# Hybrid decoder block on one core: the written order of scores and projections on TensorE, and who splits the weights beside them

## The chip, the cores and the metric

The kernel runs on one core of a Trainium2 chip, as one program. The metric is device time in microseconds (us) from start to end of the program. TensorE (PE in the profile) does the matmuls, VectorE (DVE), ScalarE (ACT) and GpSimd (POOL) work elementwise, and SyncE (SP) issues most transfers.

## What is computed

One layer of a decoder trunk on x of 512 tokens by 1024 channels: an input projection feeds three mixers and three gates, each mixer's output is projected, gated and summed, an output projection and a LayerNorm follow, then a squared-ReLU MLP and a second LayerNorm. The mixers are MoBA block attention (A), a chunked gated delta rule (B) and sparse attention over tokens that an indexer selects (C). The change lies in the indexer, which in the reference comes down to:

```
qi, ki, wi = columns of the input projection    # 8 heads x 64, one shared key of 64, 8 weights
ki    = layer_norm(ki)
score = sum over heads h of  wi[t,h] * scale * relu(qi[t,h] . ki[s])
top_k(score, causal) -> the tokens that query t may see in branch C
```

Everything is float32, and the matmuls reach that precision by splitting each operand into two halves.

## The kernel before

**Halves.** A weight tile (1024 x 128) comes in by a transfer on SP's queue into `wraw`, ScalarE rounds it to the high half `wh`, and `wl = wraw - wh` is the low half. `mm3` then makes three matmuls for each 128 rows of the weight, high x high, high x low and low x high: a triple (lines 92 to 94). Eight triples are one tile of projection, 128 output columns for all 512 tokens. `wraw`, `wh` and `wl` have three buffers each.

**Who subtracts.** `split` (line 76) counts its calls: each adds `share[0]` to `share[1]`, and the call at which the sum comes to 1 gives its subtraction to GpSimd and takes 1 off again. All other calls give it to VectorE. `share[0]` is 0 while x is loaded, is set to `SHARE[0]` = 0.34 at line 220 (every third call goes to GpSimd), and takes the next entries of `SHARE`, 0.67 among them, at later stages.

**Order.** A `Stream` holds the projection tiles in order: two of the indexer's queries (`qi`), two of `k_b`, two `qi`, two `k_b`, four `q_b`, then `v_b` and `z_b` in turn. `weave(steps, n)` runs a list of steps and puts the triples of the next n tiles between them, evenly. When a tile's last triple is through, its own elementwise work follows: `q_stack` for `qi` (two `qs` operations on VectorE), a convolution for `k_b` and `q_b` (three `y` operations on VectorE), and, after the fourth of a kind, a sigmoid and a product on GpSimd (line 282).

**The indexer's loop** (lines 431 to 440) has four weaves, each with one tile and six steps (two heads, three blocks of queries). A step, `index_score`, makes two matmuls into one of two `sc` banks (`q` with `kih`, line 318, then with `kil`, line 319; 256, 384 or 512 columns), ScalarE takes the ReLU into one of two `irl` buffers (line 423), and VectorE weights it and adds it to `isc` (line 428). Between two scores stand one or two triples. After the first weave come small matmuls, and rows of a bias table are sent to memory in 3 MB from ScalarE's queue (`rrep`). The key `kin` is normalised before that: variance, a power -0.5 on GpSimd (`krs`, line 264), four scalings (line 392), a transpose on TensorE, and `kih` and `kil` from it.

**Who sets the order.** The program is written as one list. A scheduler then orders each engine's instructions by its own estimates, within the dependences, so the order on an engine can differ from the written one, except in a `manual_schedule` block, where the named engines keep the written order. The loop is not in such a block before.

**Later.** The delta rule runs four chunks of a recurrence. A chunk takes norms with the power on GpSimd (`ss`), scales its output on VectorE (`o`, line 700), turns the next keys (`kn`, line 657) and gives them back to TensorE (line 662). Splits go on there at the share of that stage, and so they do in both attentions and the MLP.

Of the kernel before, what the change touches and what calls it, by code (L numbers as in the profile page):

```python
# [10 lines left out]
F32 = mybir.dt.float32  # L11
F32R = mybir.dt.float32r
AF = mybir.ActivationFunctionType
OP = mybir.AluOpType
# [5 lines left out]
NT = T // 128  # L20
# [18 lines left out]
SHARE = (0.34, 0.67, 0.67, 0.34, 0.34)  # L39
# [16 lines left out]
def hybrid_block(ctx, tc, xT, xn, wt, wva, wsm, wuk, wuv, wbr, wout, wup, wdn, relb, onehot, cmats,  # L56
                 convw, alog, dtb, gnorm, kvnorm, ikg, ikb, l1g, l1b, l2g, l2b, out):
    nc = tc.nc
    PE, DVE, ACT, POOL = nc.tensor, nc.vector, nc.scalar, nc.gpsimd
# [4 lines left out]
    const = ctx.enter_context(tc.tile_pool(name="const", bufs=1))  # L64
# [5 lines left out]
    def bank(tag):  # L70
        return ps.tile([128, 512], F32, name=tag, tag=tag, bufs=BANKS[tag])


    share = [0.0, 0.0]
# [8 lines left out]
    def load_w(src):  # L83
        raw = wp.tile([128, 1024], F32, name="wraw", bufs=3)
        nc.sync.dma_start(raw, src)
        h = wp.tile([128, 1024], F32R, name="wh", bufs=3)
        l = wp.tile([128, 1024], F32R, name="wl", bufs=3)
        split(h, l, raw)
        return h, l
# [9 lines left out]
    def load_x(u, n=2):  # L99
        raw = wp.tile([128, 1024], F32, name="wraw", bufs=3)  # L100
        for k in range(0, 2, n):
            s = slice(2 * u + k, 2 * u + k + n)
            rs = slice(512 * k, 512 * (k + n))
            nc.sync.dma_start(raw[:, rs], xT[:, 512 * s.start:512 * s.stop])
            split(xh[:, s].rearrange("p a t -> p (a t)"), xl[:, s].rearrange("p a t -> p (a t)"), raw[:, rs])
# [11 lines left out]
    class Stream:  # L117
# [27 lines left out]
        def weave(self, steps, n):  # L145
            self.taken += n
            start, end = self.pos, self.ends[self.taken - 1] if self.taken else 0.0
            for i, f in enumerate(steps):
                f()
                self.upto(start + (end - start) * (i + 1) / len(steps))  # L150
            self.upto(end)

    stream = Stream()
    weave = stream.weave
# [62 lines left out]
    load_x(1)  # L217
    load_x(2)
    load_x(3)
    share[0] = SHARE[0]  # L220

    cm = const.tile([128, len(CN), 128], F32, name="cm")
    for i, j in ((0, 4), (4, len(CN))):
# [1 line left out]
    C = {n: cm[:, i] for i, n in enumerate(CN)}  # L225
# [89 lines left out]
    def scores(q, a, k, l, i, n):  # L315
        p = bank("sc")
        ts = slice(128 * i, 128 * i + 128)
        PE.matmul(p[:, :n], q[:, a, ts], k[:, :n], start=True, stop=False)
        PE.matmul(p[:, :n], q[:, a, ts], l[:, :n], start=False, stop=True)
        return p  # L320
# [5 lines left out]
    def t5_rows():  # L326


        rrow = ip.tile([16, NR], F32, name="rrow", bufs=1)
        p = bank("sc")  # L330
        PE.matmul(p[:16, :NR], rbt, ohs, start=True, stop=True)
        ACT.activation(rrow, p[:16, :NR], AF.Copy, bias=0.0, scale=-1.0)
        nc.scalar.dma_start(rrep, rrow[:, None, :].to_broadcast([16, 128, NR]))
# [5 lines left out]
    p = bank("pj")  # L339
# [6 lines left out]
    p = bank("tr")  # L346
# [28 lines left out]
    la = gat[:, 5]  # L375
# [15 lines left out]
    for i in range(NT):  # L391
        DVE.tensor_scalar(kin[:, i, :64], sm[:, i, :64], kag[:, i, 0:1], krs[:, i:i + 1],
                          op0=OP.subtract, op1=OP.mult)
# [4 lines left out]
    p = bank("tr")  # L398
# [20 lines left out]
    def index_score(h, i):  # L419
        n = 128 * (i + 1)  # L420
        p = scores(qis[h // 2], h % 2, kih, kil, i, n)
        rl = ip.tile([128, T], F32, name="irl")
        ACT.activation(rl[:, :n], p[:, :n], AF.Relu)
        w = wis[:, i, h:h + 1]
        if h == 0:
            DVE.tensor_scalar(isc[i], rl[:, :n], w, None, op0=OP.mult)
        else:
            DVE.scalar_tensor_tensor(isc[i], rl[:, :n], w, isc[i], op0=OP.mult, op1=OP.add)

    weave([], 1)  # L430
    for j in range(4):
        weave([lambda h=h, i=i: index_score(h, i) for h in (2 * j, 2 * j + 1) for i in range(1, NT)], 1)
        if j == 0:
            p = bank("tr")
            PE.matmul(p[:, 0:16], C["le"], la, start=True, stop=True)
            PE.matmul(p[:, 16:32], C["gt"], la, start=True, stop=True)
            ege = const.tile([128, 3, 16], F32, name="ege")
            ACT.activation(ege[:, 0:2].rearrange("p a c -> p (a c)"), p[:, :32], AF.Exp)
            DVE.tensor_scalar(ege[:, 2], ege[:, 0], -1.0, None, op0=OP.mult)
            t5_rows()  # L440


    weave([], 4)
# [546 lines left out]
    def hid():  # L990
        return (fin.tile([128, T], F32R, name="hh", bufs=KH + 1), fin.tile([128, T], F32R, name="hl", bufs=KH + 1))
# [23 lines left out]
    for k in range(8):  # L1015
        if k < 3:
            h, l = load_w(wout[k])
# [4 lines left out]
        for a in range(2):  # L1022
            h, l = hid()
# [60 lines left out]
    for half in range(2):  # L1084
# [13 lines left out]
        for f in range(f0, KH):  # L1098
            w = load_w(wup[half * KH + f])
            p = bank("pj")  # L1100
            up_cols(p, w, 0, T)
            hid_t.append(act2(p))
        for a in range(2):
# [44 lines left out]
            for t in range(NT):  # L1148
                ts = slice(128 * t, 128 * t + 128)
                n = 512 // len(pd[t])  # L1150
                for i, p in enumerate(pd[t]):
                    for k in range(8):
                        h = hid_t[2 * lead + k]
# [78 lines left out]
```

## Time and profile before

| | us |
|---|---|
| time, median of 3 runs | 986.3 (986.23 to 987.13) |
| the profiled execution, its own time | 987.62 |
| its span in the trace | 985.8 |
| TensorE busy | 957.7 |
| VectorE, ScalarE, GpSimd busy | 548.6, 429.5, 282.3 |

The mean clock granted to TensorE in the profiled execution is 0.994 of full speed. A row of a timeline reads: start, duration, engine, line, operation, output <- inputs, shape, count, and in brackets how long the engine stood idle just before and what ended that. Matmuls overlap each other in the records, so the distance of two starts, not the duration, says what one takes.

### The profile page before, as it was taken

The numbers are of one execution on the slowest core, as the hardware profiler recorded it, in microseconds if no ns is written. First come the engines' busy times: TensorE is split into PE (matmuls) and PEld (weight loads), VectorE is DVE, ScalarE is ACT, GpSimd is POOL, SyncE is SP. The second block draws the span as 40 slices with busy tenths as digits, with TensorE's granted clock in tenths as the row PEclk, the third lists the DMA queues.
The fourth block names the chain that finished last, engine by engine and source line by source line (L and its number), as shares of the span: only waits on it lengthen the run. The fifth ranks groups of instructions, "written<-read, shape, count | busy, mean of one in ns | idle before, by whom it ended". The sixth has DMA issues, their size and how long they took to land.

```text
span 985.8 us, 12962 instructions
## 1 busy us (share of the span) xinstructions
PE 957.7 (97%) x4868; PEld 791.5 (80%) x4868; DVE 548.6 (56%) x1108; ACT 429.5 (44%) x780; POOL 282.3 (29%) x190
## 2 busy tenths in 40 slices
PE   7999999999989999999999999999999999999997
PEld 4768888887878888877878878988888888888886
DVE  4966648778988556687766666732313123231327
ACT  4445446433224766888863440244421214342210
POOL 0202335300123233255436241154320123432011
PEclk9999999999999999999999999999999999999999
DMA  6375322342113522434436554333232223232322
GB/s 203 129 106 146 112 86 67 126 149 97 44 55 107 150 70 75 113 92 113 128 109 203 181 177 177 107 109 106 89 103 90 103 86 107 88 105 88 105 64 86
DMA packets 39211, 109.65 MB, mean 111 GB/s; under 512 B 5324, under 2 KB 10093, under 8 KB 39149
## 3 DMA queue, kind: packets, MB, share of 16 engines
q1 hardware_dynamic: 37084, 105.69, 32.8%
q10 hardware_dynamic: 2064, 3.15, 2.6%
q8 instruction: 38, 0.62, 0.3%
q14 instruction: 25, 0.20, 0.1%
HBM read 93.09 MB, written 11.53 MB: 106 GB/s over the span
## 4 chain that ended last, share of the span: by engine, by line
PE 60%; DVE 5%; ACT 3%; issue 1%; POOL 0%; DMA 0%; DVEq 0%; ACTq 0%; POOLq 0%
PE pj L92 14%; PE pj L94 14%; PE pj L93 14%; PE sc L92 2%; PE sc L94 2%; PE sc L93 2%; PE tr L92 1%; PE tr L94 1%; PE tr L93 1%; PE tr L778 1%; PE ov L92 1%; PE ov L93 1%; PE ov L94 1%; ACT wh L77 1%; PE ov L797 1%
## 5 line engine op out<-in xcount | busy, mean ns | idle before, releaser
L77 ACT CAST wh<-wraw 128x1024 fp32r<-128x1024 f32 (+2 forms) x144 | 147.8, 1026 | 207.6 <-PE pj L93 85.6
L81 POOL TENSOR_TENSOR wl<-wraw,wh 128x1024 fp32r<-128x1024 f32 (+2 forms) x50 | 116.3, 2326 | 295.5 <-ACT wh L77 295.3
L81 DVE TENSOR_TENSOR wl<-wraw,wh 128x1024 fp32r<-128x1024 f32 (+2 forms) x94 | 116.5, 1241 | 149.2 <-ACT wh L77 148.8
L92 PE MATMUL pj<-xh,wh 128*128 128x512 f32 (+1 forms) x472 | 192.9, 409 | 0.6 <-ACT xh L77 0.3
L94 PE MATMUL pj<-xh,wl 128*128 128x512 f32 (+1 forms) x472 | 186.5, 395 | 2.4 <-DVE wl L81 2.4
L93 PE MATMUL pj<-xl,wh 128*128 128x512 f32 (+1 forms) x472 | 186.0, 394 | 1.8 <-DVE xl L81 1.8
L94 PEld LDWEIGHTS pj<-xh,wl 128*128 128x128 f32 (+1 forms) x472 | 88.7, 188 | 23.1 <-DVE wl L81 3.7
L92 PE MATMUL pj<-x1h,wh 128*128 128x512 f32 (+1 forms) x280 | 104.0, 371 | 0.0
L93 PE MATMUL pj<-x1l,wh 128*128 128x512 f32 (+1 forms) x280 | 103.8, 371 | 0.0
L94 PE MATMUL pj<-x1h,wl 128*128 128x512 f32 (+1 forms) x280 | 103.8, 371 | 0.0
L93 PEld LDWEIGHTS pj<-xl,wh 128*128 128x128 f32 (+1 forms) x472 | 88.9, 188 | 17.2 <-DVE xl L81 3.9
L92 PEld LDWEIGHTS pj<-xh,wh 128*128 128x128 f32 (+1 forms) x472 | 88.8, 189 | 17.2 <-ACT xh L77 1.6
L1081 DVE TENSOR_TENSOR hl<-hraw,hh 128x512 fp32r<-128x512 f32 x32 | 22.2, 692 | 108.3 <-ACT hh L1080 108.3
L1078 POOL TENSOR_TENSOR hraw<-hraw 128x512 f32<-128x512 f32 x32 | 44.3, 1384 | 60.2 <-ACT hraw L1077 60.2
L94 PEld LDWEIGHTS pj<-x1h,wl 128*128 128x128 f32 x280 | 52.7, 188 | 9.1
L93 PEld LDWEIGHTS pj<-x1l,wh 128*128 128x128 f32 x280 | 52.7, 188 | 9.0
L92 PEld LDWEIGHTS pj<-x1h,wh 128*128 128x128 f32 x280 | 52.7, 188 | 9.0
L1080 ACT CAST hh<-hraw 128x512 fp32r<-128x512 f32 x32 | 19.9, 622 | 70.2 <-POOL hraw L1078 70.2
L763 ACT ACTIVATE P<-P,ast 128x128 f32<-128x128 f32 (+1 forms) x64 | 36.1, 564 | 19.5 <-DVE ast L762 19.1
L784 DVE TENSOR_TENSOR ptl<-tr,pth 128x128 fp32r<-128x128 f32 (+1 forms) x64 | 31.1, 487 | 10.0 <-ACT pth L783 9.1
L758 POOL TENSOR_TENSOR bm<-strip,isc 128x256 f32<-128x256 f32 (+2 forms) x24 | 26.2, 1094 | 30.3 <-DVE ast L762 20.2
L778 PE MATMUL tr<-cm,P 128*128 128x128 f32 x160 | 28.2, 275 | 1.4 <-DVE ast L764 1.3
(373 smaller groups left out, 1955.0 us busy)
## 6 DMA issues: line engine op xcount, KB each, us to landing
wraw<-in_wt_dram SPq DMA_DIRECT2D x58, 512.0 KB, 3.4
wraw<-in_wup_dram SPq DMA_DIRECT2D x32, 512.0 KB, 3.3
wraw<-in_wdn_dram SPq DMA_DIRECT2D x32, 512.0 KB, 3.3
gdram<-gate SPq DMA_DIRECT2D x24, 256.0 KB, 2.0
wraw<-in_wbr_dram SPq DMA_DIRECT2D x12, 512.0 KB, 3.7
g<-gdram SPq DMA_DIRECT2D x24, 256.0 KB, 2.9
khl<-khl SPq DMA_DIRECT2D x16, 256.0 KB, 3.7
wraw<-in_wout_dram SPq DMA_DIRECT2D x8, 512.0 KB, 3.8
```

Source lines behind the costliest of these rows:

```text
L77: ACT.copy(h, raw)
L81: eng.tensor_tensor(l, raw, h.bitcast(F32), OP.subtract)
L92: PE.matmul(out_ap, lh, rh, start=first, stop=False)
L93: PE.matmul(out_ap, lh, rl, start=False, stop=False)
L94: PE.matmul(out_ap, ll, rh, start=False, stop=last)
L758: POOL.tensor_tensor(bm[:, :n], bias, self.masks[i], OP.add)
L763: ACT.activation(P, P, AF.Exp, bias=mi[:, 0:1], scale=-1.0, accum_out=mi[:, 2:3])
L778: PE.transpose(pt[:, 128 * j:128 * j + 128], self.P[:, c:c + 128], ident)
L784: DVE.tensor_tensor(dest(self.ptl), pv, dest(self.pth).bitcast(F32), OP.subtract)
L1078: POOL.tensor_tensor(a, a, a, OP.mult)
L1080: ACT.copy(th, a)
L1081: DVE.tensor_tensor(tl, a, th.bitcast(F32), OP.subtract)
```

## The change

Two edits. The indexer's loop goes into a `manual_schedule` block for TensorE, so that TensorE keeps the order in which scores and triples are written. And the line that sets the share to 0.34 moves from behind the loads of x to behind the loop: the splits that are called in between (eight of them) all go to VectorE. Lines of the changed kernel stand one lower than before up to the loop, and two higher behind it.

```diff
     load_x(3)
-    share[0] = SHARE[0]
...
     weave([], 1)
-    for j in range(4):
-        weave([lambda h=h, i=i: index_score(h, i) for h in (2 * j, 2 * j + 1) for i in range(1, NT)], 1)
-        if j == 0:
...
+    with tc.manual_schedule(engines={mybir.EngineType.PE}):
+        for j in range(4):
+            weave([lambda h=h, i=i: index_score(h, i) for h in (2 * j, 2 * j + 1) for i in range(1, NT)], 1)
+            if j == 0:
...
+                t5_rows()
+    share[0] = SHARE[0]
```

TensorE in the loop, before, where scores come again after thirteen triples without any (`sc` is a score's bank, `pj` the bank of a tile of projection):

```order
L318 MATMUL sc<-kih,qs 128x256
L319 MATMUL sc<-kil,qs 128x256
L318 MATMUL sc<-kih,qs 128x384
L319 MATMUL sc<-kil,qs 128x384
L92 MATMUL pj<-xh,wh 128x512
L318 MATMUL sc<-kih,qs 128x512
L319 MATMUL sc<-kil,qs 128x512
L93 MATMUL pj<-xl,wh 128x512
L318 MATMUL sc<-kih,qs 128x256
L319 MATMUL sc<-kil,qs 128x256
L94 MATMUL pj<-xh,wl 128x512
```

The same stretch of the changed kernel:

```order
L317 MATMUL sc<-kih,qs 128x384
L318 MATMUL sc<-kil,qs 128x384
L92 MATMUL pj<-xh,wh 128x512
L93 MATMUL pj<-xl,wh 128x512
L94 MATMUL pj<-xh,wl 128x512
L317 MATMUL sc<-kih,qs 128x512
L318 MATMUL sc<-kil,qs 128x512
L92 MATMUL pj<-xh,wh 128x512
L93 MATMUL pj<-xl,wh 128x512
L94 MATMUL pj<-xh,wl 128x512
L317 MATMUL sc<-kih,qs 128x256
L318 MATMUL sc<-kil,qs 128x256
```

Before, nine scores stood ahead of the thirteen triples and fifteen behind them, with single projection matmuls between; now whole triples stand between any two scores, all along the loop.

VectorE ahead of the loop, before, at the key's normalisation (`rs_v` is the variance that GpSimd's power reads, `kin` the scaled key, `gat` and `wis` small operands of other work):

```order
L373 TENSOR_SCALAR gat<-gat 128x16
L263 TENSOR_SCALAR rs_v<-kag 128x4
L406 TENSOR_SCALAR wis<-sm 128x32
L392 TENSOR_SCALAR kin<-sm,kag,krs 128x64 x3
L364 TENSOR_SCALAR gat<-gat 128x16
```

The same place in the changed kernel:

```order
L372 TENSOR_SCALAR gat<-gat 128x16
L262 TENSOR_SCALAR rs_v<-kag 128x4
L81 TENSOR_TENSOR wl<-wraw,wh 128x1024
L391 TENSOR_SCALAR kin<-sm,kag,krs 128x64
L363 TENSOR_SCALAR gat<-gat 128x16
```

A split that stood on GpSimd ahead of the power now stands on VectorE between `rs_v` and the scaling.

GpSimd in the recurrence, before (`ss` is the power of a chunk, `Sd` the decayed state):

```order
L684 TENSOR_TENSOR Sd<-S,el 128x512
L264 TENSOR_TENSOR ss<-rs_v,cvals 128x4
L684 TENSOR_TENSOR Sd<-S,el 128x512
L264 TENSOR_TENSOR ss<-rs_v,cvals 128x4
L81 TENSOR_TENSOR wl<-wraw,wh 128x1024
L264 TENSOR_TENSOR ss<-rs_v,cvals 128x4
L81 TENSOR_TENSOR wl<-wraw,wh 128x1024
L264 TENSOR_TENSOR ss<-rs_v,cvals 128x4
```

GpSimd in the recurrence of the changed kernel:

```order
L81 TENSOR_TENSOR wl<-wraw,wh 128x1024
L686 TENSOR_TENSOR Sd<-S,el 128x512
L263 TENSOR_TENSOR ss<-rs_v,cvals 128x4
L686 TENSOR_TENSOR Sd<-S,el 128x512
L263 TENSOR_TENSOR ss<-rs_v,cvals 128x4 x2
L81 TENSOR_TENSOR wl<-wraw,wh 128x1024
L263 TENSOR_TENSOR ss<-rs_v,cvals 128x4
```

The count of `split` reaches 1 at other calls from the loop on, so one split now stands ahead of the first `Sd`, and none between the second and the third `ss`; the one between the third and the fourth stays. Over the whole program 51 of 163 splits stand on GpSimd, where it was 54.

## Rows read from the trace of the kernel before

**Rows 1.** The page, busy time (share of the span) and instructions of each engine.

```profile
PE 957.7 (97%) x4868; PEld 791.5 (80%) x4868; DVE 548.6 (56%) x1108; ACT 429.5 (44%) x780; POOL 282.3 (29%) x190
```

**Rows 2.** Stretches: length, busy PE, PEld, DVE, ACT, POOL, PEclk, DMA share, GB/s.

```profile
70.00:80.00 10.00, 9.71 (x39) 8.03 (x39) 8.09 (x14) 5.80 (x12) 0.00 (x0) 0.83 0.90 104
280.00:290.00 10.00, 9.46 (x57) 8.60 (x58) 8.65 (x18) 2.21 (x9) 0.00 (x0) 0.83 0.33 107
300.00:590.00 290.00, 283.33 (x1495) 235.24 (x1494) 195.01 (x441) 190.14 (x402) 108.29 (x79) 1.00 0.41 125
```

**Rows 3.** Timeline of TensorE in the indexer's loop.

```profile
42.27 0.39 PE L319 MATMUL sc<-kil,qs 128*128 128x256 f32 x1 [1.38 <-DVE kil L404]
...
63.02 0.39 PE L93 MATMUL pj<-xl,wh 128*128 128x512 f32 x1
63.25 0.39 PE L94 MATMUL pj<-xh,wl 128*128 128x512 f32 x1
...
63.59 0.28 PE L319 MATMUL sc<-kil,qs 128*128 128x256 f32 x1
63.70 0.34 PE L318 MATMUL sc<-kih,qs 128*128 128x384 f32 x1
63.88 0.34 PE L319 MATMUL sc<-kil,qs 128*128 128x384 f32 x1
64.06 0.39 PE L92 MATMUL pj<-xh,wh 128*128 128x512 f32 x1
...
70.29 0.79 PE L318 MATMUL sc<-kih,qs 128*128 128x512 f32 x1 [1.75 <-ACT irl L423]
...
73.81 0.34 PE L318 MATMUL sc<-kih,qs 128*128 128x384 f32 x1
```

**Rows 4.** Timelines of GpSimd, VectorE and ScalarE, 66.9 to 70 us.

```profile
66.97 2.37 POOL L81 TENSOR_TENSOR wl<-wraw,wh 128x1024 fp32r<-128x1024 f32 x1 [22.57 <-ACT wh L77]
...
66.98 3.43 DVE L428 SCALAR_TENSOR_TENSOR isc<-irl,wis,isc 128x384 f32<-128x384 f32 x2
...
69.85 0.39 ACT L423 ACTIVATE irl<-sc 128x256 f32<-128x256 f32 x1 [1.99 <-DVE isc L428]
```

**Rows 5.** Single lines' instructions: durations in ns (least/median/most), first and last start.

```profile
L428 DVE SCALAR_TENSOR_TENSOR isc<-irl,wis,isc x21: 476/619/2770, 49.1 to 82.9; 128x256 f32<-128x256 f32 x7, 128x384 f32<-128x384 f32 x7, 128x512 f32<-128x512 f32 x7
...
L271 DVE SCALAR_TENSOR_TENSOR y_k_b<-pj,cw,y_k_b x12: 735/746/750, 40.8 to 84.4; 128x511 f32<-128x511 f32 x4, 128x510 f32<-128x510 f32 x4, 128x509 f32<-128x509 f32 x4
...
L700 DVE TENSOR_TENSOR o<-o,ss x4: 693/776/2828, 267.0 to 298.3; 128x512 f32<-128x512 f32 x4
```

**Rows 6.** Groups by line and shape: count | busy us, mean ns | idle before.

```profile
L81 DVE TENSOR_TENSOR wl<-wraw,wh 128x1024 fp32r<-128x1024 f32 x90 | 113.3, 1260 | 145.0 <-ACT wh L77 144.6 <-issue 0.2
L81 POOL TENSOR_TENSOR wl<-wraw,wh 128x1024 fp32r<-128x1024 f32 x47 | 113.0, 2404 | 286.3 <-ACT wh L77 286.1
```

**Rows 7.** Timelines of GpSimd and VectorE, 27 to 31 us.

```profile
27.14 2.40 POOL L81 TENSOR_TENSOR wl<-wraw,wh 128x1024 fp32r<-128x1024 f32 x1 [16.22 <-ACT wh L77]
29.72 1.02 POOL L264 TENSOR_TENSOR krs<-rs_v,cvals 128x4 f32<-128x4 f32 x1 [0.18 <-DVE rs_v L263]
...
27.68 1.89 DVE L373 TENSOR_SCALAR gat<-gat 128x16 f32<-128x16 f32 x1
...
30.78 0.76 DVE L392 TENSOR_SCALAR kin<-sm,kag,krs 128x64 f32<-128x64 f32 x3 [1.05 <-POOL krs L264]
```

**Rows 8.** Timelines of GpSimd, VectorE and TensorE in the recurrence.

```profile
276.99 2.35 POOL L81 TENSOR_TENSOR wl<-wraw,wh 128x1024 fp32r<-128x1024 f32 x1
...
277.06 2.83 DVE L700 TENSOR_TENSOR o<-o,ss 128x512 f32<-128x512 f32 x1 [0.53 <-POOL ss L264]
...
280.54 1.16 PE L662 MATMUL tr<-Y,kn 128*128 128x128 f32 x8 [2.46 <-DVE kn L657]
```

**Rows 9.** Transfers issued from 40 to 100 us: count, KB each, us to landing.

```profile
rrep<-rrow ACTq DMA_DIRECT2D x1, 3072.0 KB, 33.8
```

**Rows 10.** Timeline of GpSimd behind the loop.

```profile
89.18 4.63 POOL L282 TENSOR_TENSOR y_k_b<-y_k_b,sg 128x2048 f32<-128x2048 f32 x1 [19.84 <-ACT sg L281]
```

More of the change, by code (lines that the diff above doesn't have):

```diff
@@ L430, in hybrid_block @@
     weave([], 1)
-    for j in range(4):
-        weave([lambda h=h, i=i: index_score(h, i) for h in (2 * j, 2 * j + 1) for i in range(1, NT)], 1)
-        if j == 0:
[L434 to L440, printed above, removed]
+    with tc.manual_schedule(engines={mybir.EngineType.PE}):
+        for j in range(4):
+            weave([lambda h=h, i=i: index_score(h, i) for h in (2 * j, 2 * j + 1) for i in range(1, NT)], 1)
+            if j == 0:
+                p = bank("tr")
+                PE.matmul(p[:, 0:16], C["le"], la, start=True, stop=True)
+                PE.matmul(p[:, 16:32], C["gt"], la, start=True, stop=True)
+                ege = const.tile([128, 3, 16], F32, name="ege")
+                ACT.activation(ege[:, 0:2].rearrange("p a c -> p (a c)"), p[:, :32], AF.Exp)
+                DVE.tensor_scalar(ege[:, 2], ege[:, 0], -1.0, None, op0=OP.mult)
+                t5_rows()
+    share[0] = SHARE[0]
     weave([], 4)
```

## The prediction, made before the changed kernel ran

> **What bounds the kernel now.** I read the busy line first. TensorE is busy for 957.7 us of a span of 985.8 [rows 1], so the most that any change of order or of helpers can give is some 28 us, and it gives that only where TensorE stands still or runs slowly. The work on TensorE is the same before and after: the same matmuls in another order. So the question is which of those 28 us the two edits touch, and whether they make new ones. The stretches say where to look: from 70 to 80 us and from 280 to 290 the granted clock is 0.83, and from 300 to 590 it is 1.00 with TensorE busy for 283.33 of 290, so only 6.7 us are lost there over many small waits [rows 2]. A clock of 0.83 over 10 us means that some 3.4 us were run at 1.2 GHz and the rest at 2.4: 10 x (1 - 0.83) = 1.7 us were lost by it each time. Then come the timelines around these two places.
>
> *In the loop.* TensorE's timeline gives the normal distance of two starts: 0.23 us for 512 columns (63.02 to 63.25), 0.18 for 384 (63.70 to 63.88), 0.11 for 256 (63.59 to 63.70) [rows 3]. From 64.06 to 73.81 it starts 23 matmuls, 17 of 512 columns, 2 of 384 and 4 of 256. At the normal distance these take 17 x 0.23 + 2 x 0.18 + 4 x 0.11 = 4.7 us; they took 9.75, so 5.0 us are lost. Of these, 1.75 is one idle stretch that ends at 70.29, and 1.7 is the low clock that follows it; the rest are shorter waits for the same thing. The chain behind it: at 66.97 GpSimd begins a weight split of 2.37 us, and VectorE's two `isc` operations at 66.98 take 3.43 us together, where the median of one is 0.62 and the longest is 2.77 [rows 4, 5]. So VectorE was held while GpSimd ran. ScalarE waited 1.99 us for an `irl` buffer, and TensorE for an `sc` bank. It hurts so much because thirteen triples had gone out without a score, and the fifteen remaining scores were then packed with one to four projection matmuls between them, which is too little to cover VectorE's part of a score.
>
> *In the recurrence.* A split of 2.35 us starts on GpSimd at 276.99, VectorE's `o` at 277.06 takes 2.83 us instead of 0.69, `kn` behind it is late, and TensorE idles 2.46 us before 280.54 [rows 5, 8]. With the 1.7 us of clock that follows [rows 2], that one split costs 4.2 us.
>
> **The change part by part.** *Written order in the loop, with the split of 66.97 on VectorE.* The scores are spread again, and the GpSimd split that started the chain is gone. I check whether VectorE keeps up. A weave is 24 projection matmuls (24 x 0.23 = 5.5 us) and twelve of scores (4 x (0.23 + 0.18 + 0.11) = 2.1), 7.6 us of TensorE. VectorE has in it six `isc` (6 x 0.62 = 3.7), one split at its own price of 1.26 [rows 6], and three convolution steps (3 x 0.75 = 2.2) [rows 5] when the tile before was of `k_b`, or two `qs` steps when it was of `qi`: 7.2 us at most, and less in fact, since durations in the records overlap somewhat. That fits, narrowly. Its longest burst without a score is a split and a convolution, 1.26 + 2.2 = 3.5 us. Two `sc` banks and two `irl` buffers let TensorE run four scores ahead of `isc`, four sixths of a weave or 5 us, so the burst is covered. I take the whole 5.0 us as gained; the bounds are 0 (the chain turns up elsewhere in the loop) and 5.0, and I take the upper end because both causes, the packed scores and GpSimd's split, are taken away. A middle value would need a third cause, for which no row speaks.
>
> *The first score's wait.* At 42.27 TensorE waits 1.38 us for `kil` [rows 3]. Upstream, a GpSimd split at 27.14 held VectorE's `gat` for 1.89 us, pushed GpSimd's power `krs` to 29.72, and VectorE then idled 1.05 us for it [rows 7]. That split is now on VectorE, between `rs_v` and the scaling, where it fills the time in which VectorE waited. VectorE saves 1.7 us of being held and 1.05 of waiting, and pays 1.26. So the key is 0.4 (if the wait for the power stays) to 1.5 us earlier. Bounds 0 and 1.4; I take 1.0, the middle of 0.4 and 1.5, since no row shows whether the power still ends last.
>
> The rows show VectorE held by GpSimd; none shows the reverse. The Trainium skill, "SBUF — State Buffer", section "Who interferes with whom", says that the port which the two share is an exclusive lock: whichever starts first has it for its whole instruction, and the other is blocked. By that rule, VectorE's split that starts right behind `rs_v` would hold GpSimd's power for about 1.1 us, this term would shrink to some 0.4, and the sum to 9.4.
>
> *The recurrence.* The count of splits is shifted, and no split stands any more between the second and the third `ss`, where the one of 276.99 stood. The split between the third and the fourth was there before as well; of the four `o` operations only one was long (776 ns median, 2828 most) [rows 5], so that place is harmless. The new one ahead of the first `Sd` has no `ss` near it. The split that was taken from GpSimd costs VectorE 1.26 us beside its own work, of which little is on the path. Gain 4.2 - 0.2 = 4.0. Bounds: 4.2, and 0 if the split meets another operation on the path.
>
> *All else.* Behind 300 us the turns of GpSimd fall on other calls. The stretch loses 6.7 us in all to 590, so a shift can gain perhaps 2 and lose about as much as one more meeting; I take 0, with 2 either way. Three splits more on VectorE and less on GpSimd are 3.8 us on an engine that is busy for 56%, hidden by TensorE.
>
> **The sum.** 5.0 + 1.0 + 4.0 = 10.0 us, against the profiled execution's 987.6: 977.6. That execution is 1.3 above the median of the runs, so on the median it is 986.3 - 10.0 = 976.3. The bounds of the terms give 986.3 - 5.0 - 1.4 - 4.2 - 2 = 973.7 at the one end, and 986.3 - 5.0 - 0 - 4.0 + 2 = 979.3 at the other if the two large terms hold; where one falls, it is a rival.
>
> **The rivals.**
>
> (a) *The recurrence's collision moves rather than goes.* A split that is moved may meet a short VectorE operation at another chunk. One such meeting has a price of 4.2 us [rows 2, 8], so the time is 986.3 - 6.0 = 980.3. Against it: the order on GpSimd shows none next to an `ss` that was not there already. For it: the times at which splits start depend on the loads, and TensorE is some 6 us earlier than before.
>
> (b) *The gain in the loop is lost behind it, to weights that come late.* The 3 MB of `rrep` take 33.8 us to land [rows 9], and from 70 to 80 us the transfer engines are 0.90 busy [rows 2]; the loop ends 6 us sooner, while that transfer ends when it did, and tiles are then taken every 5.5 us. Besides, a split on GpSimd that comes behind the product of 4.63 us [rows 10] waits for it. TensorE would wait for weights by 2 to 5 us: 978 to 981. Against it: three buffers, and no wait of TensorE for weights at that place before.
>
> (c) *More than expected.* Smaller waits of the same kind, outside the windows I costed, go too: another 3 us or more, 973 or less. The 6.7 us of the later stretch leave room for it.
>
> (d) *Slower: the written order ties projections to VectorE.* Now that TensorE may not run ahead with triples when a score is not ready, a VectorE that falls behind stops everything. If VectorE's part of a weave is longer than TensorE's 7.6 us, the burst is no longer covered, and each of the four weaves meets one stall like that of 70.29, 1.75 us and 1.7 of clock [rows 2, 3]: 4 x 3.5 = 14 us in place of the 5.0 lost now. With the first score's 1.0 that is 986.3 - 5.0 - 1.0 + 14 = 994.3 if the recurrence keeps its collision, and 990.3 if not. It decides at 7.6 us against my 7.2, so it is near; against it, TensorE has four scores of slack, and the 7.2 leave out that durations overlap.
>
> (e) *The change does not do what it says in time:* the scheduler's order was only one outcome of an imbalance, the loop's 5.0 us stay, and the recurrence's place is hit again: 986.3 - 1.0 = 985.3, within what can be told from no change (0.2%, or 2 us).
>
> **How the numbers follow.** The forecast, 973.5 to 979.5, has a chance of 0.55; (a) 0.15; (b) 0.14; (c) 0.06; (d) 0.05; (e) 0.05. The likeliest time is 976.3. The range is to hold 8 in 10: the forecast with (a) and most of (b) is 0.55 + 0.15 + 0.12, so it runs from 972.8 to 981.5. Faster by more than 0.2% are the forecast, (a), (b) and (c), 0.90; within 0.2% is (e), 0.05; slower (d), 0.05.
>
> **What would show each step right or wrong.** In the loop, no VectorE `isc` much longer than 0.75 us, no idle of TensorE over 1 us before a score, and a granted clock of 1.00 from 60 to 80 us. Before the loop, the wait for `kil` under 0.5 us. From 270 to 300 us, four `o` of 0.7 to 0.8 us and no wait of TensorE for `kn` over 1 us. If the loop is clean and the time is over 980, the first thing to look at is TensorE's waits for `wl` and `wh` from 75 to 110 us, then the low-clock stretches from 260 to 300. The prediction is wrong in its main step if the loop is clean and TensorE's busy time is longer by what it idled less, that is if the idle stretches only covered a lower clock elsewhere.

## The result, and the profile after

The changed kernel takes 978.1 us (median of 4 runs, 977.78 to 978.78) against 986.26 for the kernel before (4 runs, 985.77 to 987.13); the ratio is 0.9923, with a 95% interval of 0.9911 to 0.9935. On a second occasion it was 978.24 against 985.41, ratio 0.9929 (0.9916 to 0.9943). So the change gains 7 to 8 us. The forecast was 976.3 in a range of 972.8 to 981.5.

The page's busy line of the changed kernel, to be read against [rows 1]: TensorE's work is the same, its busy time 3.6 us shorter, and 2.8 us have left GpSimd.

```profile
PE 954.1 (98%) x4868; PEld 791.2 (81%) x4868; DVE 549.1 (56%) x1111; ACT 428.9 (44%) x780; POOL 279.5 (29%) x187
```

Stretches of the changed kernel, with the columns of [rows 2]:

```profile
0.00:20.00 20.00, 17.06 (x52) 11.34 (x53) 9.06 (x19) 8.21 (x10) 1.07 (x7) 0.91 0.73 228
...
60.00:70.00 10.00, 10.00 (x50) 8.49 (x49) 8.57 (x15) 5.45 (x11) 0.00 (x0) 1.00 0.90 104
70.00:80.00 10.00, 10.00 (x46) 8.26 (x45) 5.24 (x8) 6.29 (x8) 0.40 (x1) 1.00 0.95 202
270.00:280.00 10.00, 9.68 (x71) 8.76 (x70) 9.75 (x21) 2.20 (x9) 0.36 (x2) 1.00 0.16 52
...
300.00:590.00 290.00, 282.68 (x1475) 233.96 (x1474) 189.25 (x424) 187.44 (x400) 110.36 (x80) 1.00 0.42 132
```

From 60 to 80 us TensorE is never idle and the clock is whole; the loop is clean. In the recurrence the wait of 2.46 us of [rows 8] has shrunk to 0.32. From 300 to 590 TensorE loses 7.3 us, where it lost 6.7. And there is a stretch of lower clock in the first 20 us that the profiled execution of before did not have.

TensorE's timeline in the loop and the recurrence (line 318 is now the matmul with `kil`, line 664 the keys' transpose):

```profile
40.00 0.28 PE L317 MATMUL sc<-kih,qs 128*128 128x256 f32 x1
40.11 0.28 PE L318 MATMUL sc<-kil,qs 128*128 128x256 f32 x1
...
271.56 1.16 PE L664 MATMUL tr<-Y,kn 128*128 128x128 f32 x8 [0.32 <-DVE kn L659]
```

The first `kil` matmul follows at 0.11 us, with no wait (1.38 in [rows 3]). Two single lines of VectorE, as in [rows 5], show that no `isc` and no `o` is held any more:

```profile
L427 DVE SCALAR_TENSOR_TENSOR isc<-irl,wis,isc x21: 477/618/754, 46.4 to 71.8; 128x256 f32<-128x256 f32 x7, 128x384 f32<-128x384 f32 x7, 128x512 f32<-128x512 f32 x7
...
L702 DVE TENSOR_TENSOR o<-o,ss x4: 692/692/860, 260.2 to 287.7; 128x512 f32<-128x512 f32 x4
```

Where the time came from is best read by taking the start of the same matmul in both traces. Each row of this table is one:

| matmul | before, us | after, us | after is ahead by |
|---|---|---|---|
| the key's transpose (line 400, now 399) | 34.69 | 34.09 | 0.60 |
| first score with `kil` | 42.27 | 40.11 | 2.16 |
| the bias rows, after the first weave (331, 330) | 50.63 | 48.06 | 2.57 |
| first decay product (482, 484) | 146.01 | 138.30 | 7.71 |
| last chunk's scores (522, 524) | 175.30 | 168.46 | 6.84 |
| first transpose of keys in the recurrence (662, 664) | 260.64 | 253.81 | 6.83 |
| last transpose of outputs there (706, 708) | 299.17 | 288.65 | 10.52 |
| first attention score | 317.57 | 307.05 | 10.52 |
| first matmul of the MLP that follows | 589.45 | 579.71 | 9.74 |
| last matmul | 978.25 | 968.51 | 9.74 |

The differences of the last column are the pieces: 0.60 at the start, 1.56 at the first score and 0.41 in the first weave, 5.14 in the loop, -0.87 between 146 and 175 us, 3.69 in the recurrence, and -0.78 in the attentions. The start is no effect of the change: up to the key's transpose TensorE's order is the same, and the kernels below are there between 0.15 and 1.03 us ahead of the one trace of before.

### The profile page after: what moved, and what is told of

It is laid out like the page before. It is cut to its first block, busy times and chain, and to the rows that moved or that the text cites. A ratio compares the mean times of both kernels' runs of the same rounds, so it can differ in the third digit from the quotient of the medians.

```text
span 976.1 us, 12981 instructions
## 1 busy us (share of the span) xinstructions
PE 954.1 (98%) x4868; PEld 791.2 (81%) x4868; DVE 549.1 (56%) x1111; ACT 428.9 (44%) x780; POOL 279.5 (29%) x187
## 4 chain that ended last, share of the span: by engine, by line
PE 61%; DVE 5%; ACT 4%; issue 1%; POOL 0%; DMA 0%; DVEq 0%; ACTq 0%; POOLq 0%
PE pj L92 15%; PE pj L94 15%; PE pj L93 14%; PE sc L93 2%; PE sc L92 2%; PE sc L94 2%; PE tr L93 1%; PE tr L92 1%; PE tr L94 1%; PE tr L780 1%; PE ov L93 1%; PE ov L92 1%; PE ov L94 1%; ACT wh L77 1%; PE ov L799 1%
## 5 line engine op out<-in xcount | busy, mean ns | idle before, releaser
L81 DVE TENSOR_TENSOR wl<-wraw,wh 128x1024 fp32r<-128x1024 f32 (+2 forms) x98 | 124.7, 1274 | 154.5 <-ACT wh L77 154.2
L81 POOL TENSOR_TENSOR wl<-wraw,wh 128x1024 fp32r<-128x1024 f32 (+1 forms) x46 | 112.4, 2447 | 309.3 <-ACT wh L77 291.1
```

The costliest lines, as they stand in the source:

```text
L81: eng.tensor_tensor(l, raw, h.bitcast(F32), OP.subtract)
```

## The experiments

All are cut into the same pieces, from their own traces against that of before, beside the median time. Each kernel differs from the kernel before or from the changed one by the lines shown. Where `share[2]` appears, it is a third entry of `share` that starts at 0 and counts the calls of `split`. The column of the loop runs from the bias rows to the first decay product; in the changed kernel all of its gain is there by 82 us of the time before, about where the loop ends.

| kernel | start | first score and first weave | loop | 146 to 175 | recurrence | 300 to 590 | median, us | ratio to before |
|---|---|---|---|---|---|---|---|---|
| changed | 0.60 | 1.97 | 5.14 | -0.87 | 3.69 | -0.78 | 978.1 | 0.9923 (0.9911 to 0.9935) |
| order_only | 0.43 | 0.03 | 4.96 | 0.0 | 1.58 | 0.1 | 980.59 | 0.9953 (0.9941 to 0.9966) |
| splits_only | 0.50 | 1.96 | 3.13 | -0.88 | 3.72 | -0.78 | 980.05 | 0.9946 (0.9933 to 0.9958) |
| one_split | 0.92 | 0.04 | 3.14 | 0.0 | 1.56 | -0.3 | 984.19 | 0.9982 (0.9973 to 0.9991) |
| old_turns | 1.03 | 1.95 | 4.96 | 0.0 | -0.31 | 0.0 | 979.98 | 0.9940 (0.9927 to 0.9954) |
| turns_only | 0.63 | 0.04 | 0.99 | -0.92 | 3.73 | -0.75 | 984.84 | 0.9995 (0.9986 to 1.0004) |
| key_split | 0.25 | 0.38 | 5.14 | -0.84 | 3.72 | -0.78 | 980.02 | 0.9945 (0.9933 to 0.9958) |
| old_turns_but_one | 0.15 | 1.96 | 4.96 | 0.0 | 3.71 | 0.1 | 976.76 | 0.9911 (0.9897 to 0.9924) |

**The written order alone.** The share line goes back to where it was.

```diff
     load_x(3)
+    share[0] = SHARE[0]
...
                 t5_rows()
-    share[0] = SHARE[0]
```

> TensorE keeps the written order in the loop; the share line stays where it was, so all splits are on the engines of the kernel before. Theory P (the packed scores are what makes the loop's stall): four scores of slack cover a GpSimd split of 2.4 us, no idle of TensorE over 0.5 us before a score from 45 to 80 us, the loop gains its 5.0 us, the wait of 1.4 us for kil and the recurrence's collision stay: 986.3 - 5.0 = 981.3. Theory G (GpSimd's split is): VectorE held for 2.4 us stalls TensorE in any order, at a place where it may not run ahead: an idle stretch of 1 us or more before a score, 984 or more.

980.59 us, and the loop's piece is 4.96: theory P holds, the order alone takes away the whole stall. A GpSimd split still falls into the loop. GpSimd and VectorE of this kernel there:

```profile
67.47 2.40 POOL L81 TENSOR_TENSOR wl<-wraw,wh 128x1024 fp32r<-128x1024 f32 x1 [23.53 <-ACT wh L77]
```

```profile
68.00 0.75 DVE L271 SCALAR_TENSOR_TENSOR y_k_b<-pj,cw,y_k_b 128x511 f32<-128x511 f32 x1 [0.79 <-ACT y_k_b L269]
68.67 1.49 DVE L428 SCALAR_TENSOR_TENSOR isc<-irl,wis,isc 128x256 f32<-128x256 f32 x1
```

The `isc` of 256 columns takes 1.49 us instead of 0.48, but TensorE has triples to issue and does not wait. The split began beside a convolution that it did not hold up, so it held an `isc` for 1.0 us here, and not for the 2.2 us of before (2.77 against 0.62 [rows 5]). Whether the order covers a hold of that length too is not shown. The wait for `kil` is there (1.35 us), and so is the one in the recurrence. TensorE's timeline, and the stretch around it:

```profile
275.14 1.16 PE L664 MATMUL tr<-Y,kn 128*128 128x128 f32 x8 [2.45 <-DVE kn L659]
```

```profile
270.00:280.00 10.00, 7.55 (x54) 6.71 (x53) 9.47 (x17) 0.60 (x2) 3.32 (x2) 1.00 0.15 53
```

The same idle as in [rows 8], but the clock stays at 1.00, and by that alone the piece gains 1.58.

**The moved splits alone.** The loop stands outside the `manual_schedule` block, the share line where the change puts it.

```diff
-    with tc.manual_schedule(engines={mybir.EngineType.PE}):
+    if True:
```

> Only the share line moves; TensorE's order is that of the kernel before. Theory P: the scores still come packed after thirteen triples, VectorE has its own split of 1.26 us there instead of being held for 2.4, so a shorter stall of about 1 us stays, and perhaps the low clock; loop +2 instead of +5.0, kil and recurrence as in the changed kernel: 978.1 + 3 = 981. Theory G: the loop is clean, 978 to 979.

980.05 us. TensorE's order in the loop is that of before, and its waits for a score's bank are two:

```profile
62.23 0.50 PE L317 MATMUL sc<-kih,qs 128*128 128x512 f32 x1 [0.24 <-ACT irl L422]
63.55 0.39 PE L317 MATMUL sc<-kih,qs 128*128 128x256 f32 x1 [0.36 <-ACT irl L422]
```

The wait of 1.75 us is gone with its low clock, so the loop gains 3.13, not 2 and not 5.0: without the held VectorE the packed scores still cost 1.8 us (the starts of TensorE's matmuls in the loop are that much further apart than at the normal distances, the two waits above among them). Neither theory is quite right: the packing alone makes short waits, and the large stall takes the packing and the split together.

**One split alone.** The kernel before, with the sixteenth call's subtraction on VectorE and the count kept.

```diff
         share[1] -= eng is POOL
+        share[2] += 1
+        if share[2] == 16:
+            eng = DVE
```

> The kernel before, with one subtraction alone (the sixteenth split, GpSimd at 66.97 us) on VectorE; order and all other splits as before. Theory P: a stall of about 1 us stays in the loop, 986.3 - 2 = 984 or more. Theory G: the loop gains 5.0: 981.3. In both the wait for kil (1.4 us) and the collision in the recurrence (2.5 us idle) are there as before.

984.19 us, and 3.14 in the loop: the same as with all the moved splits. So that part of the loop's gain hangs on the one split of 66.97 us [rows 4]. By the medians it is worth 1.4 us only, less than the traces' 3.1; the profiled execution of before is one in which the low clock followed, and not every execution is (below, where that clock comes to 0.99 of the 3.14). The recurrence has its idle of before without the low clock, as in order_only:

```profile
276.48 1.16 PE L665 MATMUL tr<-Y,kn 128*128 128x128 f32 x8 [2.46 <-DVE kn L660]
```

```profile
270.00:280.00 10.00, 7.54 (x55) 6.73 (x54) 9.47 (x19) 1.84 (x8) 3.32 (x2) 1.00 0.16 53
280.00:290.00 10.00, 9.65 (x67) 8.60 (x66) 9.31 (x20) 3.69 (x14) 1.99 (x2) 1.00 0.16 55
```

**The old turns behind the loop.** The changed kernel, with the count set so that the later GpSimd turns are those of before.

```diff
     share[0] = SHARE[0]
+    share[1] = -0.28
```

> The changed kernel, with the count of splits set behind the loop so that from the seventeenth split on the same ones as before stand on GpSimd. If the turn of a split is what makes the recurrence's collision: o of 2.8 us and an idle stretch of 2.5 us before the keys' transpose come back (+3.7 us) and the 1.7 us that the changed kernel loses at 157 to 167 us and from 300 to 590 go: 978.1 + 2.0 = 980.1. If it is the time at which loads come, the recurrence stays clean: 977 to 978.

979.98 us, as the first theory has it. GpSimd, VectorE and TensorE in the recurrence of this kernel:

```profile
269.06 2.35 POOL L81 TENSOR_TENSOR wl<-wraw,wh 128x1024 fp32r<-128x1024 f32 x1
```

```profile
269.12 2.83 DVE L703 TENSOR_TENSOR o<-o,ss 128x512 f32<-128x512 f32 x1 [0.53 <-POOL ss L263]
```

```profile
272.61 1.68 PE L665 MATMUL tr<-Y,kn 128*128 128x128 f32 x8 [2.44 <-DVE kn L660]
```

```profile
270.00:280.00 10.00, 7.56 (x44) 6.73 (x43) 9.13 (x16) 0.75 (x2) 1.41 (x1) 0.83 0.17 55
```

The collision of [rows 8] is back 8 us earlier, to within two hundredths of a microsecond in its parts, and here the low clock follows it. The losses at 146 to 175 us and from 300 on are gone. So the turn of a split, not the time at which weights come, sets both.

**The new turns alone.** The kernel before, its first sixteen splits as they were, then the turns of the changed kernel.

```diff
     def split(h, l, raw):
         ACT.copy(h, raw)
+        share[2] += 1
+        share[1] += 0.28 if share[2] == 17 else 0.0
         share[1] += share[0]
```

> The kernel before, order and first sixteen splits as before, and from the seventeenth on the turns of the changed kernel. The loop's stall and the wait for kil stay; the recurrence's idle of 2.46 us goes, 0.9 us are lost at 157 to 174 us and 0.8 from 300 to 590. If the turns act by themselves: 2.46 + up to 1.7 of clock - 1.7 = 0.8 to 2.5 gained, about 984. If the recurrence needs the earlier arrival that the loop's gain brings: no gain, 986 to 987.

984.84 us, ratio 0.9995 with 1 inside the interval. In the trace the recurrence gains its 3.73 and the other two places lose their 0.92 and 0.75, so the turns act by themselves; that net gain of 2.1 is not found in the medians, by which it is under 1.4 us. Some 1.6 of the 3.73 are the low clock of before: order_only and one_split are ahead by that much there with the same idle. TensorE's one large wait in this kernel's loop, and the two stretches around it:

```profile
69.61 0.50 PE L320 MATMUL sc<-kih,qs 128*128 128x512 f32 x1 [1.76 <-ACT irl L425]
```

```profile
60.00:70.00 10.00, 7.64 (x34) 5.28 (x33) 5.94 (x6) 4.72 (x9) 2.37 (x1) 1.00 0.89 104
70.00:80.00 10.00, 10.00 (x47) 7.43 (x46) 8.96 (x15) 6.22 (x13) 0.00 (x0) 1.00 0.90 107
```

The stall of [rows 3] is there, with 1.76 us for 1.75, and no lower clock after it. That alone puts the loop's piece at 0.99. So the low clock, which cost TensorE 1.7 us, was worth 1.0 to the loop: at the full clock TensorE meets some 0.7 us of short waits (by the distances of its starts) behind the stall that it does not have in the trace of before.

**The key's split.** The changed kernel, with the tenth call's subtraction back on GpSimd.

```diff
         share[1] -= eng is POOL
+        if share[2] == 10:
+            eng = POOL
```

> The changed kernel with one subtraction, the tenth split, on GpSimd as before. If this one makes the wait for kil: TensorE waits some 1.4 us before the first kil matmul, GpSimd's power takes 1.0 us instead of 1.9, 978.1 + 1.4 = 979.5. If the other moved splits make it: 978.

980.02 us, 1.9 more than the changed kernel by the medians of two occasions, 1.6 by the pieces of the traces. GpSimd around the key, and TensorE's first scores:

```profile
26.86 2.40 POOL L84 TENSOR_TENSOR wl<-wraw,wh 128x1024 fp32r<-128x1024 f32 x1 [15.62 <-ACT wh L77]
29.44 1.02 POOL L266 TENSOR_TENSOR krs<-rs_v,cvals 128x4 f32<-128x4 f32 x1 [0.18 <-DVE rs_v L265]
```

```profile
41.97 0.39 PE L321 MATMUL sc<-kil,qs 128*128 128x256 f32 x1 [1.32 <-DVE kil L406]
```

The wait is back, so this one split makes it. The changed kernel's GpSimd at the same place, and its VectorE, show what the split does now:

```profile
27.38 1.93 POOL L263 TENSOR_TENSOR krs<-rs_v,cvals 128x4 f32<-128x4 f32 x1 [16.29 <-DVE rs_v L262]
```

```profile
27.21 1.22 DVE L81 TENSOR_TENSOR wl<-wraw,wh 128x1024 fp32r<-128x1024 f32 x1
29.35 0.32 DVE L391 TENSOR_SCALAR kin<-sm,kag,krs 128x64 f32<-128x64 f32 x1 [0.92 <-POOL krs L263]
```

GpSimd's power starts at 27.38, while VectorE subtracts until 28.43, and takes 1.93 us instead of 1.02.

**The old turns but one.** The changed kernel with the old turns, and the forty-fifth call's subtraction, the one of 276.99 us in [rows 8], on VectorE.

```diff
     share[0] = SHARE[0]
+    share[1] = -0.28
...
         share[1] -= eng is POOL
+        if share[2] == 45:
+            eng = DVE
```

> The changed kernel with the turns of before from the seventeenth split on, except the forty-fifth, the one that met o in the recurrence, which is put on VectorE. If the collision is this one split, and the changed kernel's 1.7 us lost at 157 to 174 us and behind 300 come from the other turns: recurrence clean, no loss behind it, 978.1 - 1.7 = 976.4, faster than the changed kernel. If the collision moves to another operation: 979 to 980 as with the old turns.

976.76 us: the recurrence is clean (3.71) and nothing is lost elsewhere. This version and the changed kernel ran once more, beside each other:

> The changed kernel once more, beside the version with the old turns but one on the same chip. If that version is better by the 1.7 us that the traces show behind the recurrence and at 157 to 174 us: 978 here and 976.5 there, the intervals apart. If the difference lay between the chips or in the clock: both within 0.5 us.

> The version with the old turns but one, beside the changed kernel on the same chip: 976.5 if the turns are what it gains by, 978 if not.

978.24 us (977.93 to 978.45) for the changed kernel and 976.75 (976.61 to 978.3) for the other, ratios 0.9929 (0.9916 to 0.9943) and 0.9918 (0.9904 to 0.9932). The medians are apart by 1.5 us here and by 1.3 (976.76 against 978.1) the first time, but the two intervals overlap, where the expectation had them apart: one execution of the better one came to 978.3, with a mean clock of 0.994 where its others have 0.997 to 0.999. The traces bear the difference out: the two places where the changed kernel loses 0.87 and 0.78 are clean. It is the best version here.

In the changed kernel of this run, the first 20 us have a clock of 1.00:

```profile
0.00:20.00 20.00, 15.67 (x53) 10.10 (x54) 8.89 (x19) 8.07 (x10) 1.07 (x7) 1.00 0.72 228
```

So the 0.91 there in the profile above is of that execution, not of the program.

## Why the prediction was right, point by point

**What bounds it, and where to look.** Right. The two places with a clock of 0.83 and an idle stretch in front were the two large gains.

**The loop, 5.0.** Measured 5.14 in the trace. The reason given, two causes that are both taken away, holds, but they are not two shares of a sum: the order alone gives 4.96, the splits alone 3.13, both 5.14. And there was a third part, which is not the program's: of the 5.0 us, 1.8 are the packed scores by themselves (one_split still has them), 1.0 is the low clock (turns_only), and the other 2.2 are the stall that the split adds. The check of VectorE's load was right in its result; rival (d) did not come, and order_only shows that the four scores of slack even cover an `isc` that GpSimd holds up for 1 us; a longer hold was not met.

**The first score, 1.0 of bounds 0 and 1.4.** Undersized, and above its bound: 1.56, and 0.41 more in the first weave. The rule of the Trainium skill, "SBUF — State Buffer", "Who interferes with whom", came true: GpSimd was held by VectorE, for 0.9 us by the rows above, which no row of before had shown. The time that followed from it (a term of 0.4) did not come. The split was rightly named (key_split), but the way from it to `kil` was not the one of the prediction. The key `kin` does not come earlier. VectorE's last step of it, and TensorE's transposes of it, before:

```profile
32.80 0.29 DVE L396 COPY kin<-kin 128x256 f32<-128x256 f32 x1
...
34.69 0.60 PE L400 MATMUL tr<-cm,kin 128*128 128x128 f32 x4
```

and in the changed kernel:

```profile
33.64 0.29 DVE L395 COPY kin<-kin 128x256 f32<-128x256 f32 x1
...
34.09 0.60 PE L399 MATMUL tr<-cm,kin 128*128 128x128 f32 x4
```

The step comes 0.8 us later, and the transposes wait in neither kernel and are ahead by the start's 0.60 alone. What comes earlier is VectorE's turn for `kil`, which stands behind its other work: `kil` starts at 39.06 instead of 41.53, which is 1.9 us ahead without the start. Of these, 1.75 are there at `rs_v` already (27.14 against 29.49), since no split holds `gat`. From `rs_v` to `kil` VectorE then takes 11.92 us against 12.04, although it has one split more, which lies in the time before the power is there, with the small operations behind it in another order. So the 1.26 that the prediction subtracted were not paid. Of the 0.41 in the first weave, 0.32 stay in key_split and none in order_only; they belong to the other split that has left GpSimd there, the one that started at 42.02 and held this step of VectorE for 2.17 us, where the changed kernel takes 0.69 (40.48):

```profile
42.79 2.17 DVE L479 TENSOR_TENSOR R<-cm,lahl 128x512 fp32r<-128x512 f32 x1
```

**The recurrence, 4.0.** In the trace 3.69, and old_turns and old_turns_but_one show that it is this one split. Rival (a) did not come. But the term was mis-sized as a gain of the median. It took 1.7 us of low clock as belonging to the idle stretch. Four traces have this idle of 2.45 us: before, order_only, one_split and old_turns. The clock fell behind it in the first and the last (0.83) and stayed at 1.00 in the other two. The stall in the loop was followed by 0.83 in the trace of before, and by 1.00 in turns_only. The low clock is worth 1.58 and 1.56 there, as order_only and one_split show, so the recurrence's gain is 2.1 us against an execution of before without it, and 3.7 against one with it.

**All else, 0 with 2 either way.** Measured -0.87 and -0.78, a loss of 1.65 near the lower bound. It is the price of the shifted turns: all four kernels with the new turns lose 0.84 to 0.92 at the first place and 0.75 to 0.78 at the second, and those with the old nothing at the first and at most 0.3 (one_split) at the second. The forecast had put the term at nothing. TensorE's waits from 300 to 590 in the changed kernel, line and releaser, total us, times, longest:

```profile
PE tr L780 <- DVE ast L766: 3.2, 4, 1.3
```

and the same in old_turns_but_one:

```profile
PE tr L784 <- DVE ast L770: 1.3, 4, 0.4
```

The waits for `ast`, a step of the softmax on VectorE, have grown from 1.3 to 3.2 us in sum, where others have gone. Which split meets which operation there was not followed.

**The sum.** 5.0 + 1.0 + 4.0 = 10.0 was forecast; the two traces are 9.74 apart, the medians 8.2. That the traces come so near to 10.0 is partly luck: the first score and the first weave gave 0.97 more than forecast and the start 0.60, and the shifted turns took 1.65. The 9.74 also hold two falls of the clock in before's execution that not every execution has. Without the start the pieces sum to 9.1, and without the two falls (0.99 and some 1.57) to 6.6; the medians of the two occasions, 8.2 and 7.2, lie between. The step that was weak is thus the last one: one execution's low-clock stretches were carried over to the median as if the program made them. Of the kernel before, beside the first four experiments, 15 executions took 983.68 to 986.75 us at mean clocks of 0.999 to 0.994; the profiled one, 987.62 at 0.994, is slower than all of them.

**The other rivals.** (b): TensorE does not wait from 60 to 100 us, so the weights were not late; (c) did not come; (e): both edits do what they say.

## What to carry to other kernels

Where another engine has work to do behind each small matmul, spread those matmuls evenly among the long ones and pin that order: here it took away the whole loss of the loop by itself, and covered the other engine when it was 1 us late. Work that is dealt out by a running count moves every later deal when an earlier one is changed, so look at the whole program, and then fix single deals by hand; here one deal was worth 3.2 us (old_turns against old_turns_but_one, by the medians). Idle stretches may be taken from one trace, but a low clock behind them only at a discount.

## What the runs showed of the hardware

A lower clock does not follow every idle stretch of the same length. After an idle of 2.44 to 2.46 us in the same place of the same matmuls it fell to 1.2 GHz for some 3.4 us in two traces of four (an estimate from the clock of 0.83 over 10 us), and not at all in the other two, which were 1.58 and 1.56 us faster there than before. The Trainium skill, "TensorE: Matmul & The Clock Gate", section "Part 1: The HAM clock gate (the "warmup" mystery)", says that the chip looks at TensorE's activity by a time of its own that does not start with the kernel. The rows agree with that, but do not prove it.

VectorE and GpSimd hold each other up in both directions: a subtraction on GpSimd makes VectorE's `o` 2.83 us instead of 0.69, and one on VectorE makes GpSimd's power 1.93 instead of 1.02. In one place (order_only, 68.00) a convolution step that reads one operand from PSUM (`pj`) and one from SBUF took its ordinary 0.75 us under a GpSimd subtraction, while the `isc` behind it, with both from SBUF, took 1.49 instead of 0.48.
